# Keeping the two halves of a weight unit in one buffer, and spacing the five buffers by 64 bytes modulo 512

## The chip, the cores and the metric

The kernel runs on one core of one Trainium2 chip. The metric is device time in microseconds (us) of one execution; lower is better.

## The reference

Two layers act on x, 256 rows (SEQ) by 1024 columns (D_MODEL), in float32. Cut to what matters here:

```
for l in range(2):
    h = rms_norm(x, norm_mix_pre[l])
    proj = h @ w_in[l]                         # 1024 x 8224
    y_a = mla_branch(...)   @ w_o_mla[l]       # attention, 8 heads; w_uq, w_ukv inside
    y_b = short_conv_branch(...) @ w_o_sc[l]
    y_c = conformer_branch(...)  @ w_o_cf[l]   # convolution of 31 taps
    y_d = gmlp_branch(...)       @ w_o_gm[l]
    g = sigmoid(gate_logits + gate_b[l])       # four gates
    merged = g0*y_a + g1*y_b + g2*y_c + g3*y_d
    x = x + rms_norm(merged @ w_out[l], norm_mix_post[l])
    h2 = rms_norm(x, norm_ffn_pre[l])
    f_g, f_u = split(h2 @ w_ffn_in[l])         # 1024 x 5632
    x = x + rms_norm((silu(f_g) * f_u) @ w_ffn_out[l], norm_ffn_post[l])
```

## The kernel before

**Tiling.** The 256 rows are two row tiles of 128 (t = 0, 1). All weights stream once from HBM, in units of at most 128 partitions by 2048 float32 (1 MB). `Weights.load` brings a unit into a `raw` tile (4 buffers). `Weights.split` then makes two operands of it for TensorE: ScalarE casts `raw` to float32r, which is `hi`, and VectorE computes `lo = raw - hi`; both work in spans of 1024 columns, so a full unit is two casts and two subtractions. `hi` and `lo` are tiles of their own with 5 buffers each (`B_HI`). Activations are split in the same way, into `hth` and `htl` (the normed input, transposed) and pairs in the common 2 KB tiles (`slot`, 25 buffers: `fh`/`fl`, `mh`/`ml` and so on).

**Products.** `group` issues three matmuls for each 128 rows of contraction: (left hi, right hi), (left hi, right lo), (left lo, right hi). The left operand is loaded into the array, the right one streams through it. In most stages the left operand is an activation and the weights stream, 512 columns a matmul. In `b_unit` the weights are the left operand and 256 columns of `hth`/`htl` stream, so there `hi` is read by the first two matmuls of a triple and `lo` by the third. In `compressed` 272 columns of weights stream. For one layer that is 64 stretches of 24 matmuls with 512 columns (1536), 12 calls of `b_unit` with 48 (576 of 256 columns), 96 of 272 and 24 of 384: 2232, and 4464 for both layers. The other TensorE work is transposes, attention and the gMLP mixing, in plain float32.

**Order.** The order of TensorE's instructions is the order of the code; those of ScalarE, VectorE, GpSimd and SyncE are placed beside it by a planner inside the kernel (`Engine`, `event`, `pump`) from estimated costs. A unit is split when one of the five buffers has been freed (`Weights.free`, `fill`), so five units are ahead of TensorE at most. Waits between engines are derived from the tiles: the first instruction that writes into a reused buffer waits for all readers of what lay there before.

**Addresses.** Every tile starts at some byte of each partition of SBUF. In the built program the start modulo 512 is 64 for `raw`, `hi`, `lo`, `hth`, `htl`, `gain` and all `slot` tiles (`gt`, `m`, `gv`, `brow`, `f` are such tiles), 192 for `x` and the identity, and 352 for the 4 KB tiles `h` of the norms. All `hi` and `lo` buffers are 8192 bytes apart. A span of `compressed` weights starts at a step of 2176 bytes for each 128 rows of contraction and 1088 bytes for the second half, so the streaming operand there begins 0, 64, 128, 192, 256 or 320 bytes (modulo 512) behind the operand loaded into the array; in all other stages that difference is 0.

Of the kernel before, what the change touches and what calls it, by code (L numbers as in the profile page):

```python
# [12 lines left out]
F32R = mybir.dt.float32r  # L13
# [5 lines left out]
P = 128  # L19
# [12 lines left out]
EPS = 1e-6  # L32
NCOL = 148
UW = 2048
FIRST = 544

O_CQ, O_CKV, O_KR = 0, 256, 512
# [59 lines left out]
def hybrid_encoder(ctx: ExitStack, tc: tile.TileContext, wts, x_in, pos, invf, cols, rows, wst, out):  # L97
# [159 lines left out]
    wp = ctx.enter_context(tc.tile_pool(name="wp", bufs=1))  # L257
# [3 lines left out]
    B_RAW, B_HI, B_SLOT, B_BIG, B_GAIN = 4, 5, 25, 2, 2  # L261
# [7 lines left out]
    def nm(s):  # L269
        cnt[0] += 1  # L270
        return f"{s}_{cnt[0]}"
# [49 lines left out]
    class Weights:  # L321
# [4 lines left out]
        def load(self, i, t=0.0):  # L326
            l, u = divmod(i, NU)
            w, after = widths[u], t
            t = wp.tile([P, UW], F32, tag="raw", name=nm("raw"), bufs=B_RAW)
            o = (l * offs[-1] + offs[u]) * P  # L330
            src = wts[o : o + w * P].rearrange("(p w) -> p w", w=w)
            step = FIRST if i == 0 else w
            for c in range(0, w, step):
# [2 lines left out]

        def split(self, i):
            w = widths[i % NU]
            h = wp.tile([P, UW], F32R, tag="hi", name=nm("hi"), bufs=B_HI)
            lo = wp.tile([P, UW], F32R, tag="lo", name=nm("lo"), bufs=B_HI)  # L340
            raw = self.raw.pop(i)
            step = FIRST if i == 0 else 1024
            self.parts[i] = (h, lo)
            spans = [(c, min(w, c + step)) for c in range(0, w, step)]

            def rank():
                return 0 if i <= self.n + NEAR else 3

            for c, e in spans:
                act.copy(h[:, c:e], raw[:, c:e], rank=rank)  # L350
                dve.tensor_tensor(lo[:, c:e], raw[:, c:e], h[:, c:e], op=ALU.subtract, rank=rank, then=self.more if e == w else None)
# [124 lines left out]
    def pre_norm(t, g):  # L476
        h = big()
        ss = small(1)
        r = small(1)
        act.activation(h, x[:, t, :], AF.Square, scale=D ** -0.5, accum_out=ss, rank=FAST)  # L480
        rstd_of(r, ss, rank=FAST)
        for j in range(2):
            c = slice(512 * j, 512 * (j + 1))
            dve.scalar_tensor_tensor(h[:, c], x[:, t, c], r, g[:, c], op0=ALU.mult, op1=ALU.mult, rank=FAST)

        def turn():
            for j in range(2):
                yield need(h)
                b = sbank()
                transposes(b, [h[:, 512 * j + P * k : 512 * j + P * (k + 1)] for k in range(4)])  # L490
                bv = b.rearrange("p (k n) -> p k n", n=P)
                split(hth[:, t, 4 * j : 4 * j + 4, :], htl[:, t, 4 * j : 4 * j + 4, :], bv, FAST)

        return turn()
# [83 lines left out]
    def layer(l):  # L578
# [26 lines left out]
        def mla_tr(t, cn):  # L605
            yield need(cn)
            b = sbank()
            transposes(b, [cn[:, P * k : P * (k + 1)] for k in range(4)])
            for j in range(2):
                o = slice(t * P, (t + 1) * P)  # L610
                split(ft2(qc[j])[:, :, o], ft2(ql[j])[:, :, o], b[:, 256 * j : 256 * (j + 1)].rearrange("p (f n) -> p f n", f=2))
# [84 lines left out]
        def split_op(name, j, src):  # L696
            hi, lo = slot(F32R, name + "h"), slot(F32R, name + "l")
            split(hi, lo, src)
            ops[name][j] = (ft2(hi), ft2(lo))
# [481 lines left out]
```

## Time and profile before

| | |
|---|---|
| median of 2 runs | 966.59 us (966.5 to 966.67) |
| profiled execution, its own time | 966.32 us |
| its span, first to last instruction | 964.5 us |
| TensorE busy | 950.7 us (99% of the span) |
| VectorE busy | 669.5 us |
| ScalarE busy | 476.4 us |
| HBM read | 177.63 MB, 185 GB/s over the span |

The span is what the instruction records cover; 1.8 us of the execution's own time lie outside it. Busy times overlap between engines. Matmuls are pipelined: the record of one lasts longer than its share of the engine, so the rate is read from start to start.

### The profile page before, as it was taken

The numbers are of one execution on the slowest core, as the hardware profiler recorded it, in microseconds if no ns is written. First come the engines' busy times: TensorE is split into PE (matmuls) and PEld (weight loads), VectorE is DVE, ScalarE is ACT, GpSimd is POOL, SyncE is SP. The second block draws the span as 40 slices with busy tenths as digits, with TensorE's granted clock in tenths as the row PEclk, the third lists the DMA queues.
The fourth block names the chain that finished last, engine by engine and source line by source line (L and its number), as shares of the span: only waits on it lengthen the run. The fifth ranks groups of instructions, "written<-read, shape, count | busy, mean of one in ns | idle before, by whom it ended". The sixth has DMA issues, their size and how long they took to land.

```text
span 964.5 us, 12950 instructions
## 1 busy us (share of the span) xinstructions
PE 950.7 (99%) x5098; PEld 821.9 (85%) x5098; DVE 669.5 (69%) x1018; ACT 476.4 (49%) x733; POOL 44.6 (5%) x87
## 2 busy tenths in 40 slices
PE   8999999999999999999999999999999999999997
PEld 7999988888887888888899999888888878888885
DVE  6968788898857655553387888788987485555532
ACT  6656655436435644443275656544455364444421
POOL 1100000000001000000031000000000010000000
PEclk9999999999999999999999999999999999999999
DMA  9844353455844645565267144445566266455601
GB/s 365 291 164 152 114 196 142 179 212 191 321 153 156 237 180 192 195 218 180 88 239 286 56 170 161 147 177 200 213 243 233 104 236 244 175 175 187 227 0 44
DMA packets 29726, 179.52 MB, mean 186 GB/s; under 512 B 3681, under 2 KB 3809, under 8 KB 10209
## 3 DMA queue, kind: packets, MB, share of 16 engines
q1 hardware_dynamic: 29664, 178.69, 51.8%
q8 instruction: 40, 0.66, 0.3%
q14 instruction: 22, 0.17, 0.1%
HBM read 177.63 MB, written 1.05 MB: 185 GB/s over the span
## 4 chain that ended last, share of the span: by engine, by line
PE 94%; DVE 2%; ACT 1%; issue 1%; DMA 1%; POOL 1%; SPq 0%; DVEq 0%; POOLq 0%; ACTq 0%
PE pb L248 74%; PE acc L248 12%; PE psd L252 4%; PE psd L248 2%; PE av L248 1%; DVE lo L175 1%; DMA raw<-in_wts_dram 1%; POOL c L175 1%; ACT hi L175 1%; DVE h L175 0%; ACT h L175 0%; DVE x L175 0%; SPq L309 0%; DVE htl L175 0%; ACT sq L175 0%
## 5 line engine op out<-in xcount | busy, mean ns | idle before, releaser
L175 DVE TENSOR_TENSOR lo<-raw,hi 128x1024 fp32r<-128x1024 f32 (+4 forms) x321 | 374.1, 1202 | 136.3 <-ACT hi L175 136.1
L175 ACT CAST hi<-raw 128x1024 fp32r<-128x1024 f32 (+4 forms) x321 | 319.1, 1037 | 277.2 <-PE pb L248 140.6
L248 PE MATMUL pb<-hi,hth 128*128 128x512 f32 (+1 forms) x704 | 272.5, 387 | 0.8 <-ACT hth L175 0.8
L248 PE MATMUL pb<-lo,hth 128*128 128x512 f32 (+1 forms) x704 | 268.1, 381 | 3.9 <-DVE lo L175 3.9
L248 PE MATMUL pb<-hi,htl 128*128 128x512 f32 (+1 forms) x704 | 268.3, 381 | 0.7 <-DVE htl L175 0.4
L248 PEld LDWEIGHTS pb<-lo,hth 128*128 128x128 f32 x704 | 132.3, 188 | 29.1 <-DVE lo L175 5.2
L248 PEld LDWEIGHTS pb<-hi,htl 128*128 128x128 f32 x704 | 132.2, 188 | 27.2 <-DVE htl L175 2.0
L248 PEld LDWEIGHTS pb<-hi,hth 128*128 128x128 f32 x704 | 132.3, 188 | 24.8 <-ACT hth L175 1.1
L248 PE MATMUL pb<-hth,hi 128*128 128x256 f32 x384 | 109.9, 286 | 0.0
L248 PE MATMUL pb<-htl,hi 128*128 128x256 f32 x384 | 108.6, 283 | 0.0
L248 PE MATMUL pb<-hth,lo 128*128 128x256 f32 x384 | 108.6, 283 | 0.0
L175 DVE SCALAR_TENSOR_TENSOR yc<-zc,hcol,yc 128x241 f32<-128x241 f32 (+14 forms) x240 | 97.8, 472 | 0.0
L248 PEld LDWEIGHTS pb<-htl,hi 128*128 128x128 f32 x384 | 73.7, 192 | 0.3
L248 PEld LDWEIGHTS pb<-hth,hi 128*128 128x128 f32 x384 | 73.6, 192 | 0.3
L248 PEld LDWEIGHTS pb<-hth,lo 128*128 128x128 f32 x384 | 73.7, 192 | 0.0
L248 PE MATMUL acc<-hi,fh 128*128 128x512 f32 x176 | 68.8, 391 | 0.0
L248 PE MATMUL acc<-hi,fl 128*128 128x512 f32 x176 | 68.5, 389 | 0.0
L248 PE MATMUL acc<-lo,fh 128*128 128x512 f32 x176 | 68.5, 389 | 0.0
L248 PEld LDWEIGHTS acc<-hi,fl 128*128 128x128 f32 x176 | 33.0, 188 | 7.0
L248 PEld LDWEIGHTS acc<-hi,fh 128*128 128x128 f32 x176 | 33.0, 188 | 6.8
L248 PEld LDWEIGHTS acc<-lo,fh 128*128 128x128 f32 x176 | 33.0, 188 | 6.7
L175 POOL TENSOR_SCALAR c<-c 128x1 f32<-128x1 f32 (+1 forms) x20 | 12.7, 634 | 518.1 <-ACT sq L175 474.5
(161 smaller groups left out, 1007.6 us busy)
## 6 DMA issues: line engine op xcount, KB each, us to landing
raw<-in_wts_dram SPq DMA_DIRECT2D x152, 1024.0 KB, 4.8
brow<-in_rows_dram SPq DMA_DIRECT2D x24, 256.0 KB, 5.6
gain<-in_rows_dram SPq DMA_DIRECT2D x8, 512.0 KB, 6.1
raw<-in_wts_dram SPq DMA_DIRECT2D x3, 816.0 KB, 4.6
raw<-in_wts_dram SPq DMA_DIRECT2D x2, 768.0 KB, 5.8
raw<-in_wts_dram SPq DMA_DIRECT2D x2, 544.0 KB, 6.1
x<-in_x_dram SPq DMA_DIRECT2D x2, 512.0 KB, 5.9
out_dram<-x SPq DMA_DIRECT2D x4, 256.0 KB, 2.1
```

The lines of the kernel that those rows point to most:

```text
L175: o.emit = lambda: f(*a, **k)
L248: nc.tensor.matmul(out, lhsT, rhs, **k)
L252: nc.tensor.transpose(out=out, in_=in_, identity=identity)
```

## The change

`hi` and `lo` of a unit become the first and the second 2048 columns of one tile `hl` with 5 buffers. A tile is 16 columns (64 bytes) longer than the two together, 16448 bytes, which is 64 modulo 512. In the built program the five buffers start at 64, 128, 192, 256 and 320 modulo 512, and `lo` has the same residue as its `hi`, as before. `raw`, `hth`, `htl`, `x` stay where they were. What is allocated behind the buffers moves 320 bytes up: `gain` and all `slot` tiles from 64 to 384, the tiles `h` from 352 to 160.

```diff
+SHIFT = 16
@@ class Weights, split @@
-            h = wp.tile([P, UW], F32R, tag="hi", name=nm("hi"), bufs=B_HI)
-            lo = wp.tile([P, UW], F32R, tag="lo", name=nm("lo"), bufs=B_HI)
+            both = wp.tile([P, 2 * UW + SHIFT], F32R, tag="hl", name=nm("hl"), bufs=B_HI)
+            h, lo = both[:, :UW], both[:, UW : 2 * UW]
```

The order of the instructions on every engine is the same before and after. What differs is where some waits stand. ScalarE's row, in the `b_unit` stage of layer 0, before (`th` is the tanh of a `b_unit` result `pb`; the casts write weight units into reused buffers):

```order
L175 CAST hi_554<-raw_406 128x1024 [waits DVE_49,DMAHW0_49,PE_49,Activation_49]
L175 ACTIVATE th_556<-pb_485 128x512 [waits PE_49]
L175 CAST hi_554<-raw_406 128x1024
L175 ACT_TABLE_LOAD
L175 ACTIVATE sin<-ang_479 128x32 [waits DVE_49]
```

and the same place after:

```order
L176 CAST hl_544<-raw_398 128x1024 [waits DVE_49,DMAHW0_49,PE_49,Activation_49]
L176 ACTIVATE th_545<-pb_475 128x512
L176 CAST hl_544<-raw_398 128x1024
L176 ACT_TABLE_LOAD
L176 ACTIVATE sin<-ang_469 128x32 [waits DVE_49]
```

Nothing moved; the wait of `th` for TensorE is gone, because the cast ahead of it now waits for the last reader of `lo` as well, which is the last matmul of that `b_unit`. There are 8 such rows on ScalarE; 4 subtractions on VectorE lose their wait for TensorE in the same way, and 8 matmuls gain a wait of TensorE for one of its own earlier matmuls, beside the wait for ScalarE that they have in both kernels. SyncE's and GpSimd's waits are the same.

## Rows read from the trace of the kernel before

**Rows 1.** The page: span, busy times by engine, TensorE's granted clock in 40 slices.
```profile
span 964.5 us, 12950 instructions
PE 950.7 (99%) x5098; PEld 821.9 (85%) x5098; DVE 669.5 (69%) x1018; ACT 476.4 (49%) x733; POOL 44.6 (5%) x87
...
PEclk9999999999999999999999999999999999999999
```

**Rows 2.** The page: the chain that ended last, shares by engine.
```profile
PE 94%; DVE 2%; ACT 1%; issue 1%; DMA 1%; POOL 1%; SPq 0%; DVEq 0%; POOLq 0%; ACTq 0%
```

**Rows 3.** Timeline, TensorE, FFN input stage (start, length, instruction): 94 rows, first and last.
```profile
347.00 0.39 PE L248 MATMUL pb<-hi,htl 128*128 128x512 f32 x1
...
368.08 0.39 PE L248 MATMUL pb<-hi,htl 128*128 128x512 f32 x1
```

**Rows 4.** Timeline, TensorE, FFN output stage: 88 rows, first and last.
```profile
440.16 0.39 PE L248 MATMUL acc<-hi,fh 128*128 128x512 f32 x1
...
459.88 0.39 PE L248 MATMUL acc<-hi,fh 128*128 128x512 f32 x1
```

**Rows 5.** Timeline, TensorE, `b_unit` stage: 54 rows, first and last.
```profile
85.53 0.28 PE L248 MATMUL pb<-hth,lo 128*128 128x256 f32 x1
...
91.89 0.28 PE L248 MATMUL pb<-htl,hi 128*128 128x256 f32 x1
```

**Rows 6.** Timeline, TensorE, `compressed` stage of layer 1: 36 rows, first and last.
```profile
499.49 0.29 PE L248 MATMUL pb<-hi,htl 128*128 128x272 f32 x1
...
503.90 0.29 PE L248 MATMUL pb<-lo,hth 128*128 128x272 f32 x1
```

**Rows 7.** Windows: length, busy PE, PEld, DVE, ACT, POOL, clock, DMA share.
```profile
180.00:295.00 115.00, 115.00 (x529) 95.43 (x528) 90.62 (x127) 53.60 (x78) 3.44 (x9) 1.00 0.57 204
31.00:100.00 69.00, 69.00 (x520) 66.86 (x519) 56.27 (x135) 40.03 (x58) 2.77 (x4) 1.00 0.51 190
314.00:425.00 111.00, 111.00 (x510) 92.23 (x509) 63.01 (x73) 53.05 (x73) 0.00 (x0) 1.00 0.55 196
434.00:479.00 45.00, 45.00 (x200) 37.24 (x200) 16.53 (x16) 14.21 (x18) 1.09 (x4) 1.00 0.42 144
```

**Rows 8.** Groups by shape: busy us, mean ns of one | idle before it.
```profile
L175 DVE TENSOR_TENSOR lo<-raw,hi 128x1024 fp32r<-128x1024 f32 x311 | 368.6, 1220 | 136.3 <-ACT hi L175 136.1
L175 ACT CAST hi<-raw 128x1024 fp32r<-128x1024 f32 x311 | 314.1, 1052 | 275.7 <-PE pb L248 140.6 <-issue 64.1 <-PE acc L248 36.3
...
L175 DVE TENSOR_TENSOR m<-m,gt 128x512 f32<-128x512 f32 x24 | 16.5, 686 | 0.1
...
L175 DVE SCALAR_TENSOR_TENSOR x<-h,c,x 128x512 f32<-128x512 f32 x16 | 11.3, 748 | 9.3 <-POOL c L175 9.3
...
L175 ACT ACTIVATE h<-x 128x1024 f32<-128x1024 f32 x8 | 8.5, 1062 | 11.7 <-DVE x L175 9.4 <-DMA x<-in_x_dram 2.3
...
L175 DVE TENSOR_TENSOR h<-acc,gain 128x512 f32<-128x512 f32 x8 | 5.4, 690 | 25.7 <-ACT sq L175 13.5 <-PE acc L248 12.1
...
L175 DVE SCALAR_TENSOR_TENSOR gv<-gv,c,brow 128x512 f32<-128x512 f32 x4 | 3.0, 748 | 1.2 <-POOL c L175 1.2
```

**Rows 9.** Waits: who for whom, us in total, times, longest.
```profile
ACT hi L175 <- PE pb L248: 140.6, 54, 4.2
...
PE pb L248 <- DVE lo L175: 3.9, 3, 1.5
```

**Rows 10.** Timeline, GpSimd, in the norms around 300 us.
```profile
297.66 0.22 POOL L175 TENSOR_SCALAR c<-c 128x1 f32<-128x1 f32 x1 [6.13 <-ACT sq L175]
...
302.70 2.13 POOL L175 TENSOR_SCALAR c<-c 128x1 f32<-128x1 f32 x1 [3.45 <-ACT h L175]
```

**Rows 11.** Timeline, VectorE, the same place at 300 us.
```profile
301.26 3.49 DVE L175 TENSOR_TENSOR lo<-raw,hi 128x1024 fp32r<-128x1024 f32 x3
305.52 0.75 DVE L175 SCALAR_TENSOR_TENSOR h<-x,c,gain 128x512 f32<-128x512 f32 x1 [0.77 <-POOL c L175]
```

**Rows 12.** Windows, instructions on `lo` alone: PE, PEld, DVE in the gate stage.
```profile
180.00:295.00 115.00, 63.16 (x163) 30.48 (x163) 47.33 (x40) 1.00 0.57 204
```

## The prediction

> **What bounds the kernel now.** I read the page's busy times first, then its chain. TensorE is busy for 950.7 of the 964.5 us of the span, at a granted clock of 9 tenths or more in every slice, and the chain that ended last runs through TensorE for 94% of the span [rows 1, 2]. The other engines have room: VectorE 69%, ScalarE 49%. So the time can move in two ways only: the rate at which TensorE takes matmuls changes, or TensorE comes to wait more or less.
>
> The rate is read from start to start, since the records overlap. With 512 columns streaming it is (368.08 - 347.00)/93 = 226.7 ns in the FFN input stage [rows 3] and (459.88 - 440.16)/87 = 226.7 ns in the FFN output stage [rows 4]. With 256 columns it is (91.89 - 85.53)/53 = 120.0 ns [rows 5], with 272 columns (503.90 - 499.49)/35 = 126.0 ns [rows 6]. At the granted clock of 1.00 [rows 7], which is the upper level of 2.4 GHz, the columns alone take 213.3, 106.7 and 113.3 ns. A fixed 13.4, 13.3 and 12.7 ns a matmul remains, whatever the column count. Over the 4464 float32r matmuls this fixed part is some 59 us, the only large sum in the trace that an address could possibly own.
>
> Waiting is small: TensorE stood idle for VectorE's `lo` for 3.9 us in all, in 3 places [rows 9].
>
> The changed kernel's own profiled execution is compared with 966.32 us (964.5 of span and 1.8 around it); the median of the runs is 966.59, 0.3 higher, and the forecast below is given on the median's scale.
>
> **The change part by part.**
>
> *Instructions.* None is added, removed or moved: the order on each engine is the same. Sum: 0. SyncE's waits are the same too, so no load is issued in another place.
>
> *Addresses against TensorE's reads.* Four of the five buffers now start 64 to 256 bytes (modulo 512) away from `hth`, and all five away from the `slot` tiles, where before everything lay at 64. The trace of before has a stage with just such distances: in `compressed` the streaming operand is 0 to 320 bytes off the loaded one, and there the fixed part is 12.7 ns instead of 13.3 to 13.4. So a distance is worth at most 0.6 to 0.7 ns a matmul, 0.65 x 4464 = 2.9 us. I take 0: starts are recorded with a few ns of rounding, 272 columns is a third size, and a mean over 35 matmuls at six distances that still lies within 1 ns of the rest says that the distance isn't what the 13 ns are. I keep -2.9 for the range.
>
> *Addresses against the writes of ScalarE and VectorE.* Casts and subtractions write one buffer while TensorE reads another. If they collided, the rate would depend on how much they run. In the FFN input stage VectorE is busy for 57% and ScalarE for 48% of the time, in the output stage for 37% and 32% [rows 7], and the rate is 226.7 ns in both [rows 3, 4]. Moreover a shift of the start can't keep the streams apart: a cast moves 4096 bytes in 1052 ns [rows 8], 3.9 bytes a ns, and TensorE reads 2048 in 226.7 ns, 9.0 bytes a ns, so the distance between them runs through all 512 residues every 100 ns or so, wherever they start. Sum: 0.
>
> The one contention that the trace does show has nothing to do with addresses. GpSimd's one-column addition takes 0.22 us at 297.66 and 2.13 us at 302.70 [rows 10], where three subtractions run back to back on VectorE [rows 11]. The Trainium skill, page "SBUF — State Buffer", section "Who interferes with whom", says that only the port pair which VectorE shares with GpSimd causes contention, as a lock held for a whole instruction, that a VectorE instruction with two SBUF inputs takes part in it, and that TensorE and ScalarE wait for nobody. The 2.13 against 0.22 us agrees. By that rule no address matters, which speaks against any gain of this change, and the sum stays 0.
>
> *Within one instruction.* In a subtraction `raw` stays at 64 while `hi` and `lo` move together; in a cast input and output part. Here streams go at one speed and keep their distance. Pairs of rows bound it: VectorE takes 748 ns for 512 columns with operands at 352 and 192 (`x<-h,c,x`) and 748 with all at 64 (`gv<-gv,c,brow`); 690 with output at 352 and one input in PSUM (`h<-acc,gain`) and 686 with all at 64 (`m<-m,gt`); ScalarE takes 1062 ns for 1024 columns from 192 to 352 (`h<-x`) and 1052 from 64 to 64 [rows 8]. That is 0 to 8 ns for 1024 columns on VectorE and up to 10 on ScalarE, or 2.5 and 3.1 us over 311 of each, in either direction as far as the rows can exclude it. Both engines lie beside TensorE there (in the gate stage VectorE is busy for 90.6 of 115 us), so on the path it is 0. If that cover were gone, all 2.5 us would count; I keep +2.5.
>
> *Waits.* After a `b_unit`, the cast into its buffer waits for the last reader of `lo`, one matmul of 120 ns later than the last reader of `hi`. There are 12 calls of `b_unit` a layer, 24 in all: 24 x 0.12 = 2.9 us at most, on ScalarE. Behind the cast on ScalarE stand `th` or `gu` (which need the same last matmul anyway), then the second cast; behind these the subtraction, and TensorE only five units later. ScalarE waits there for TensorE anyway (140.6 us in 54 places, rows named ACT hi), while TensorE hardly waits for `lo` [rows 9]. On the path: 0, at worst +2.9. The 8 added waits of TensorE for its own matmuls name work of an earlier use of the same bank; each stands beside a wait for ScalarE, which had to read that bank's finished sum, so it is fulfilled already. The 12 waits that go were fulfilled by the cast's own. Sum: 0.
>
> *Timing by chance.* Where GpSimd is locked out, VectorE then stands idle for 0.77 us before the norm's `h`, and TensorE is idle there too [rows 11]; the other layer has the same place. A shift of a cast by some 0.1 us could free both or lock another norm: -1.5 to +1.5 us. I take 0, since nothing in that stage moves.
>
> Total: 0, from -2.9 - 1.5 to +2.9 + 1.5 at the bounds, and these are not likely to come together.
>
> **The rivals.**
>
> *The 13 ns are a meeting of the two operands' addresses.* With every operand at one residue, loading the next left operand might get in the way of the stream at each matmul, and the new distances would free it. Price: the 13.3 ns of all matmuls but those with `hth` and the one buffer that stays at 64; if half the matmuls use `hth` and a fifth of these keep distance 0, 0.9 x 59 = 53 us, 913 us. For it: the fixed part exists in all stages where the distance is 0. Against it: `compressed` has five other distances and the same fixed part within 0.7 ns [rows 6]. The Trainium skill, page "TensorE: Matmul & The Clock Gate", section "Wait — 56ns, not 53.3ns?", has a fixed cost of about 2.5 ns a matmul; as an estimate by that page some 11 of the 13 ns here would be avoidable, 48 us in all, and the trace doesn't agree with it for float32r in any stage.
>
> *VectorE becomes the bound (the slow side).* If a subtraction whose two inputs differ in residue had to take its columns twice, it would last 1.07 us longer (1220 - 686 = 534 ns for 512 columns more [rows 8], so 1068 ns for 1024). Place: the gate stage, with 40 subtractions in 115 us [rows 12]. It decides from (115 - 90.6)/40 = 0.61 us more per subtraction; at 1.07 us VectorE needs 90.6 + 42.8 = 133.4 us, 18.4 over, and 37 us in both layers: 1003 us. Against it: `x<-h,c,x` with two residues costs the same 748 ns as `gv<-gv,c,brow` with one.
>
> *The later cast counts in full:* 966.6 + 2.9 = 969.5 us, slower but within 2%. For it, that casts wait for TensorE at all; against it, the five units of lead.
>
> *The change doesn't separate what meets.* `hi` and `lo` keep one common residue, and the buffer being written differs from the one being read by 64 bytes that the two speeds run through anyway. Then the time is that of the forecast; I count it there.
>
> **How the numbers follow.** Likeliest is no change, 966.6 us, with its bounds 0.86. The gain on TensorE's fixed part has 0.03, and a smaller gain of some us that no row shows 0.04; the later cast or a slightly slower rate beyond the bound has 0.05; VectorE as the bound 0.02. The range is the forecast's own, 2.9 us to either side, which leaves out less than 2 in 10: 963.7 to 969.5. A run of this kernel can tell some 2% (19 us) from no change: faster by more than that 0.03, slower 0.02, within 0.95.
>
> **What the profile after would show.** Starts 226.7, 120.0 and 126.0 ns apart in the stages of rows 3 to 6, a subtraction of 1220 and a cast of 1052 ns, and the same pieces of waiting around 300 and 775 us. A rate of 225 ns or less with 512 columns would prove the address argument wrong, in favour of the first rival. A subtraction over 1240 ns would say that the distance within an instruction costs something; TensorE waiting for `lo` more than 3.9 us, that the lead of five units was not the cover I took it for.

## The result and the profile after

The changed kernel takes 975.14 us (975.11 to 975.17, 2 runs) against 966.59 before: ratio 1.0089, 95% interval [1.0067, 1.011]. It is slower by 8.6 us, within 2% but clear of its interval and outside the forecast's range.

The page of the kernel after, span, busy times and TensorE's clock:

```profile
span 973.4 us, 12958 instructions
PE 959.5 (99%) x5098; PEld 819.3 (84%) x5098; DVE 670.2 (69%) x1018; ACT 476.2 (49%) x733; POOL 44.5 (5%) x87
...
PEclk9999999999999999999999999999999999999999
```

Against [rows 1] the span has grown by 8.9 us and TensorE's busy time by 8.8; VectorE, ScalarE and GpSimd are within 1 us, the clock is the same. So TensorE does the same work more slowly, and it doesn't wait more. The groups by shape and the waits of the kernel after say the same:

```profile
L176 DVE TENSOR_TENSOR hl<-raw,hl 128x1024 fp32r<-128x1024 f32 x311 | 368.5, 1220 | 140.2 <-ACT hl L176 139.8
L176 ACT CAST hl<-raw 128x1024 fp32r<-128x1024 f32 x311 | 313.6, 1050 | 281.5 <-PE pb L249 152.8 <-issue 65.3 <-PE acc L249 37.2
```

```profile
PE pb L249 <- DVE hl L176: 3.4, 3, 1.5
```

A subtraction takes 1220 ns as before, a cast 1050 instead of 1052 [rows 8]; TensorE waits 3.4 us for `lo` instead of 3.9 [rows 9]. GpSimd's blocked addition is still there (timeline, GpSimd):

```profile
304.41 2.13 POOL L176 TENSOR_SCALAR c<-c 128x1 f32<-128x1 f32 x1 [3.45 <-ACT h L176]
```

What changed is the time from one matmul's start to the next, and it changed from buffer to buffer. The timeline of TensorE in the FFN output stage, the first matmul of each of five units, 24 matmuls apart (a row can merge two matmuls with the same names):

```profile
433.65 0.63 PE L249 MATMUL acc<-hl,fh 128*128 128x512 f32 x2
...
439.12 0.63 PE L249 MATMUL acc<-hl,fh 128*128 128x512 f32 x2
...
444.71 0.62 PE L249 MATMUL acc<-hl,fh 128*128 128x512 f32 x2
...
450.29 0.62 PE L249 MATMUL acc<-hl,fh 128*128 128x512 f32 x2
...
455.78 0.39 PE L249 MATMUL acc<-hl,fh 128*128 128x512 f32 x1
```

These units lie in the buffers at 128, 320, 256 and 192 (modulo 512), and `fh`/`fl` at 384. The differences divided by 24 are 227.9, 232.9, 232.5 and 228.8 ns, where all of [rows 4] had 226.7. The weights, which stream, begin 0, 192, 128 and 64 bytes behind the activations, which are loaded, modulo 256. This difference of start addresses, streaming minus loaded operand, modulo 256 bytes, is called the distance below.

In `b_unit` the same happens the other way. The timeline of TensorE, the second matmul of two triples in each of three calls:

```profile
84.08 0.28 PE L249 MATMUL pb<-htl,hl 128*128 128x256 f32 x1
...
89.06 0.28 PE L249 MATMUL pb<-htl,hl 128*128 128x256 f32 x1
...
89.77 0.28 PE L249 MATMUL pb<-htl,hl 128*128 128x256 f32 x1
...
94.53 0.28 PE L249 MATMUL pb<-htl,hl 128*128 128x256 f32 x1
...
95.59 0.28 PE L249 MATMUL pb<-htl,hl 128*128 128x256 f32 x1
...
99.55 0.28 PE L249 MATMUL pb<-htl,hl 128*128 128x256 f32 x1
```

Over 42, 42 and 33 matmuls that is 118.6, 113.3 and 120.0 ns, at distances of 128, 192 and 0 bytes between the streaming `hth`/`htl` and the loaded weights; [rows 5] had 120.0.

Taken over the whole trace, each start put to the addresses of its operands in the built program (starts further apart than 260 ns with 512 columns and 150 ns with 256, which are waits and changes of stage, left out of the means):

| distance, bytes | 0 | 64 | 128 | 192 |
|---|---|---|---|---|
| 512 columns: matmuls, mean ns | 959, 228.6 | 576, 229.9 | 672, 232.3 | 864, 233.2 |
| 256 columns: matmuls, mean ns | 432, 119.9 | 192, 116.6 | 288, 118.6 | 240, 115.4 |

The distance counts, and not the tile: at 192 it is 233.4 ns with `hth` loaded and the buffer at 256, and 233.5 with `fh` loaded and the buffer at 64, where the rhythm is steady (inside a stretch of one distance, away from its ends and from waits). 256 bytes more change nothing: with `hth` loaded, steady starts lie 227.5 ns apart with the buffer at 64 and 227.3 with the buffer at 320. With 256 columns the distance alone doesn't fix the rate: of the four calls at 64, one runs at 113.3 ns and three at 117.6 to 117.9, and the mean of 116.6 is none of these. Summed start to start, the 512-column matmuls take 718.3 us instead of 707.6 (+10.7), the 256-column ones 137.3 instead of 139.4 (-2.1); the rest adds 0.3. That is the 8.9 us of the span.

### The profile page after: what moved, and what is told of

Read it like the earlier page. It is cut to its first block, busy times and chain, and to the rows that moved or that the text cites. A ratio compares the mean times of both kernels' runs of the same rounds, so it can differ in the third digit from the quotient of the medians.

```text
span 973.4 us, 12958 instructions
## 1 busy us (share of the span) xinstructions
PE 959.5 (99%) x5098; PEld 819.3 (84%) x5098; DVE 670.2 (69%) x1018; ACT 476.2 (49%) x733; POOL 44.5 (5%) x87
## 4 chain that ended last, share of the span: by engine, by line
PE 94%; DVE 2%; DMA 1%; ACT 1%; issue 1%; POOL 1%; SPq 0%; DVEq 0%; POOLq 0%; ACTq 0%
PE pb L249 74%; PE acc L249 13%; PE psd L253 4%; PE psd L249 2%; PE av L249 1%; DMA raw<-in_wts_dram 1%; DVE hl L176 1%; POOL c L176 1%; ACT hl L176 1%; DVE h L176 0%; SPq L310 0%; DVE x L176 0%; ACT h L176 0%; DVE htl L176 0%; ACT sq L176 0%
## 5 line engine op out<-in xcount | busy, mean ns | idle before, releaser
L176 DVE TENSOR_TENSOR hl<-raw,hl 128x1024 fp32r<-128x1024 f32 (+4 forms) x321 | 374.2, 1202 | 140.3 <-ACT hl L176 139.8
L176 ACT CAST hl<-raw 128x1024 fp32r<-128x1024 f32 (+4 forms) x321 | 318.6, 1035 | 283.3 <-PE pb L249 152.8
L249 PE MATMUL pb<-hl,hth 128*128 128x512 f32 (+1 forms) x1408 | 428.8, 387 | 4.6 <-DVE hl L176 3.4
L249 PEld LDWEIGHTS pb<-hl,hth 128*128 128x128 f32 x1408 | 258.1, 188 | 57.4 <-DVE hl L176 4.7
L249 PE MATMUL pb<-hl,htl 128*128 128x512 f32 (+1 forms) x704 | 270.2, 384 | 0.6 <-DVE htl L176 0.4
L249 PEld LDWEIGHTS pb<-hl,htl 128*128 128x128 f32 x704 | 132.2, 188 | 29.5 <-DVE htl L176 1.9
L249 PE MATMUL pb<-hth,hl 128*128 128x256 f32 x768 | 139.3, 282 | 0.0
L249 PEld LDWEIGHTS pb<-hth,hl 128*128 128x128 f32 x768 | 118.9, 189 | 0.3
L249 PE MATMUL acc<-hl,fh 128*128 128x512 f32 x352 | 110.2, 394 | 0.0
L249 PE MATMUL pb<-htl,hl 128*128 128x256 f32 x384 | 107.9, 281 | 0.0
```

The source lines that it names most:

```text
L176: o.emit = lambda: f(*a, **k)
L249: nc.tensor.matmul(out, lhsT, rhs, **k)
```

## The experiments

Theory A: TensorE's rate depends on the distance between the operand that streams and the operand that is loaded. Its rivals: B, the common buffer costs (later release, other waits); C, the distance between the buffer being written and the one being read costs; D, the streaming operand meets what ScalarE and VectorE write. Theory A has two forms: in A1 the operand that counts is the one being loaded for the next matmul beside the stream, in A2 it is the matmul's own, loaded before. Each time stands beside its own chip's 966.5 to 966.6 us of the kernel before.

### hi and lo in one buffer, no spacing

```diff
-SHIFT = 16
+SHIFT = 0
```

> hi and lo in one buffer, but without the 16 extra columns: all five buffers at 64 modulo 512, as hth, htl, raw and the slot tiles. Theory A (TensorE's rate depends on the distance, modulo 256 bytes, between the streaming operand and the operand loaded into the array): 966.6 us, 512-column matmuls 226.7 ns apart, 256-column ones 120.0. Theory B (the common buffer costs, through the later release of hi and the other waits): some 975 us with the rates of before.

Measured: 966.52 us, ratio 0.9999 [0.999, 1.0009]. B falls: the common buffer with all its moved waits is free, as the prediction had it. All of the loss is the spacing's. The casts of this kernel and TensorE's wait for `lo`:

```profile
L176 ACT CAST hl<-raw 128x1024 fp32r<-128x1024 f32 x311 | 314.0, 1051 | 276.2 <-PE pb L249 144.8 <-issue 64.3 <-PE acc L249 36.3
...
PE pb L249 <- DVE hl L176: 3.9, 3, 1.5
```

ScalarE stands idle 0.5 us longer before its casts than in [rows 8], and TensorE's wait for `lo` is that of [rows 9].

### All five buffers at one distance of 128 bytes

```diff
-SHIFT = 16
+SHIFT = 64
-            h, lo = both[:, :UW], both[:, UW : 2 * UW]
+            o = 32
+            h, lo = both[:, o : o + UW], both[:, UW + o : 2 * UW + o]
```

The buffers are a multiple of 256 bytes long now, so that they, the `slot` tiles and `gain` keep the residue 64 modulo 256; only `o` moves the weights.

> All five buffers at one common distance of 128 bytes (modulo 256) from hth, htl, raw and the slot tiles; nothing apart between the buffers. Theory A, from the rows of the changed kernel at this distance (232.5 ns with 512 columns, 118.6 with 256): 3072 x 5.8 ns more and 1152 x 1.4 ns less, 966.6 + 17.8 - 1.6 = 983 us. Theory C (what costs is that a buffer being written lies 64 bytes apart, modulo 512, from the one being read): 966.6 us, since the five buffers differ by multiples of 256 only. Theory B: some 975 us.

Measured: 980.69 us, ratio 1.0146 [1.0131, 1.0161]. C falls, since nothing is apart between the buffers and the loss is larger than in the changed kernel. The chain that ended last, a stretch of 96 matmuls of the FFN input stage of this kernel (start, us, what):

```profile
350.86 22.30 PE pb L249 x96
```

That is 232.3 ns a matmul. Over the trace steady rhythms have 232.5 ns with 512 columns and 119.1 with 256. The time is 2 us under the expectation; the sum of the 512-column starts grew by 15.2 us instead of 17.8, because only the 2659 steady ones grew, by 15.0 us; the other 412, near transposes, waits and changes of stage, grew by 0.2. With 256 columns 0.9 us came off instead of 1.6.

### 64 bytes for b_unit alone

```diff
+            o = 16 if units[i % NU][1:3] == (0, D) else 0
```

(with `SHIFT = 64` and the slices of the experiment before, as in all that follow; the condition picks the units that `b_unit` loads into the array.)

> Buffers at the distance 0 (modulo 256) for all units but those of b_unit, which lie 64 bytes further up in their buffer, so that the streaming hth begins 192 bytes (modulo 256) behind the loaded weights. Theory A, from the rows of the changed kernel (115.0 ns against 120.0): 1152 x 5.0 ns less, 966.6 - 5.8 = 961 us, faster than both kernels. Theories B and C: not faster than 966.6 us.

Measured: 962.39 us, ratio 0.9957 [0.9942, 0.9971]: faster than both kernels, but by 4.2 us instead of 5.8. The trace has two steady rhythms at this distance: 8 of the 24 calls of `b_unit` run at 113.3 to 114.0 ns, the others at 117.6 to 117.9. The timeline of TensorE in one call of each kind, the second matmul of the first and last triple, 45 matmuls apart:

```profile
43.49 0.28 PE L249 MATMUL pb<-htl,hl 128*128 128x256 f32 x1
...
48.79 0.28 PE L249 MATMUL pb<-htl,hl 128*128 128x256 f32 x1
...
514.77 0.28 PE L249 MATMUL pb<-htl,hl 128*128 128x256 f32 x1
...
519.87 0.28 PE L249 MATMUL pb<-htl,hl 128*128 128x256 f32 x1
```

That is 117.8 and 113.3 ns, with the same addresses modulo 256.

### Scan in steps of 16 bytes

```diff
+            o = 4 * ((i % NU + 4 * (i // NU)) % 16)
```

> A scan in one run: each unit lies 0, 16, 32 ... 240 bytes into its buffer, in turn. Theory A: the start-to-start time of the matmuls is a function of the distance modulo 256 alone, the same in every stage with that column count: with 512 columns 226.7, 229, 232.5 and 233.4 ns at 0, 64, 128 and 192 bytes, with 256 columns 120.0, 116.6, 118.6 and 115.0 at 0, 64, 128 and 192; what lies between is open. Theories B and C: no order by distance. Total about 970 us either way.

Measured: 979.16 us in one run. Steady mean ns from start to start by distance, worked out as above:

```
bytes      0    16    32    48    64    80    96   112   128   144   160   176   192   208   224   240
512 col 227.4 231.6 233.4 233.1 229.5 231.1 233.6 231.4 232.5 233.3 234.3 232.6 233.3 234.6 233.4 230.8
256 col 119.9 117.4 116.6 116.7 117.8 118.1 120.1 119.1 120.1 120.2 117.3 118.7 113.3 117.8 118.4 118.3
```

The order by distance is there and repeats the values at 64, 128 and 192 within 0.4 ns with 512 columns; with 256 columns 1.2, 1.5 and 2.1 ns of difference say that a mean hides several rhythms. The total was missed by 9 us: I had the distances between the multiples of 64 near the mean of these, and nearly all are at the upper end. With 512 columns nothing beats 0.

### htl alone moved by 128 bytes

```diff
-    htl = cp.tile([P, T, KD, P], F32R, name="htl")
+    htl = cp.tile([P, T * KD * P + 64], F32R, name="htl")[:, 32 : 32 + T * KD * P].rearrange("p (t k n) -> p t k n", t=T, k=KD)
```

> The kernel before, with htl alone moved 128 bytes (modulo 256); hth, weights and everything else keep one residue. It asks which pair meets. A triple is (hth, hi), (hth, lo), (htl, hi), loaded operand first. Theory A1 (a stream is slowed by the loading of the next matmul's operand, which runs beside it): with 512 columns the second matmul of a triple takes some 232.5 ns, the first and third 226.7. Theory A2 (a stream is slowed by its own loaded operand): the third takes 232.5, the others 226.7. Theory D (the streaming operand meets what ScalarE and VectorE write, and the loaded operand is nothing to it): 226.7 in all three. In both A1 and A2 640 matmuls get 5.8 ns more, 966.6 + 3.7 = 970 us, less up to 1 us in b_unit; in D 966.6.

Measured: 971.13 us, ratio 1.0048 [1.0025, 1.0071]. D falls: no weight buffer and no write into one has moved against another (what lies behind `htl` moved by 256 bytes). Of the triples in the stages with `hth` (523 of each place, steady) the first takes 227.1 ns, the second 232.5, the third 234.1; with the other activations all stay at 226.5 to 227.7. So A1 holds, the matmul beside which `htl` is loaded is slowed, and the one that then runs with `htl` is slowed too, as A2 has it. Whether the third is slowed by its own operand or by its slowed neighbour, this run doesn't separate; in the scan of `lo` below, matmuls are slowed whose own pair lies at distance 0. The timeline of this kernel shows how near the two are, TensorE's streams (PE) and loads (PEld):

```profile
348.33 0.40 PE L248 MATMUL pb<-hi,hth 128*128 128x512 f32 x1
348.33 0.19 PEld L248 LDWEIGHTS pb<-lo,hth 128*128 128x128 f32 x1
348.56 0.39 PE L248 MATMUL pb<-lo,hth 128*128 128x512 f32 x1
348.56 0.19 PEld L248 LDWEIGHTS pb<-hi,htl 128*128 128x128 f32 x1
348.79 0.39 PE L248 MATMUL pb<-hi,htl 128*128 128x512 f32 x1
```

The load for the next matmul starts within 4 ns of the stream of this one, in 99% of the matmuls with 512 columns. So stream and load meet in the same way at each matmul of a stretch, which would let their start addresses matter; that this is the reason is argued, not shown.

### Scan in steps of 4 bytes

```diff
+            o = (i % NU + 4 * (i // NU)) % 16
```

> A second scan: each unit lies 0, 4, 8 ... 60 bytes into its buffer. Theory A with a unit of 16 bytes: the 512-column time is one value within each group of 16 bytes, 227 ns for 0 to 12 bytes, about 231.6 at 16 to 28, 233 at 32 to 60. Theory A without such a unit: it rises from the first 4 bytes on. Total about 979 us. No step is expected below 226.

Measured: 979.68 us in one run. Steady means with 512 columns:

```
bytes      0     4     8    12    16    20    24    28    32    36    40    44    48    52    56    60
512 col 226.8 238.1 233.2 228.9 231.8 239.0 234.3 228.6 233.4 235.4 233.6 230.0 233.3 236.0 232.0 228.5
```

Three units in a row, at 0, 4 and 8 bytes, the first matmul of each, 24 matmuls apart (timeline, TensorE):

```profile
400.98 0.62 PE L249 MATMUL pb<-hl,hth 128*128 128x512 f32 x2
...
406.43 0.63 PE L249 MATMUL pb<-hl,hth 128*128 128x512 f32 x2
...
412.14 0.63 PE L249 MATMUL pb<-hl,hth 128*128 128x512 f32 x2
```

That is 227.1 ns at 0 and 237.9 at 4. A group of 16 bytes doesn't have one value: within each 16 bytes it falls from 4 to 12, by 9 to 10 ns in the first two groups and 5 to 8 in the others. Again 0 is best. With 256 columns the lowest mean was 113.7 ns, at 52 bytes up in the buffer (distance 204).

### Scan of lo's distance

```diff
+            o = 16 if units[i % NU][1:3] == (0, D) else 0
+            q = max(o, 4 * ((i % NU + 4 * (i // NU)) % 16))
+            h, lo = both[:, o : o + UW], both[:, UW + q : 2 * UW + q]
```

> hi lies as in the kernel with 64 bytes for b_unit alone, lo lies 0, 16 ... 240 bytes further (from 64 on in b_unit). Theory A1 or A2: with 512 columns only one or two matmuls of a triple change with lo's distance, to 231 to 234 ns; total 962.4 + some 1000 matmuls x 6 ns = 968 us. If some combination of unequal distances runs under 226 ns with 512 columns or holds 113.3 ns with 256, it shows here.

Measured: 976.77 us in one run, 9 over the expectation. With 512 columns all three matmuls of a triple grow in most distances (at 48 bytes to 233.0, 237.3 and 234.1 ns), although `hi` lies at 0: a displaced `lo` spoils its neighbours' rhythm too. No triple's mean is under the 227.3 of distance 0. In `b_unit`, with `hi` 64 and `lo` 192 bytes up, a triple averages 114.1 ns in one call.

### 52 bytes for b_unit

`o = 13` instead of 16 in the third experiment.

> As the kernel with 64 bytes for b_unit alone, but 52 bytes instead of 64, so that the streaming hth begins 204 bytes (modulo 256) behind the loaded weights; all other units at distance 0. In the scan of 4-byte steps this distance held 113.7 ns in all its rows, where 192 bytes switched between 113.3 and 117.8. Theory A: 1152 x (120.0 - 113.7) = 7.3 us less than before, 959.3 us, and 3 us less than with 64 bytes. If the 113 ns were only a matter of how the stage is entered, it gives about the 962.4 us of 64 bytes.

Measured: 964.84 us, ratio 0.9977 [0.9968, 0.9987]: theory A's 959.3 us failed, and the 962.4 of the other expectation was missed too. One distance again gives two rhythms, as the doubt in its last sentence had it. The timeline of TensorE in two calls of this kernel, the second matmul of the first and last triple counted:

```profile
90.48 0.28 PE L249 MATMUL pb<-htl,hl 128*128 128x256 f32 x1
...
95.16 0.28 PE L249 MATMUL pb<-htl,hl 128*128 128x256 f32 x1
...
112.74 0.28 PE L249 MATMUL pb<-htl,hl 128*128 128x256 f32 x1
...
115.83 0.28 PE L249 MATMUL pb<-htl,hl 128*128 128x256 f32 x1
```

39 matmuls at 120.0 ns, 27 at 114.4 (the first few of these still settle, the rest run at 113.3), at one and the same distance. 18 of the 24 calls hold the slow rhythm. The ten runs fall into two lots as well, 963.2 to 963.4 and 964.7 to 965.2 us.

### 8 bytes for b_unit

`o = 2`.

> As the kernel with 64 bytes for b_unit alone, with 8 bytes instead: the streaming hth begins 248 bytes (modulo 256) behind the loaded weights. In the scan of 4-byte steps this distance gave 115.6 ns in its two calls of b_unit, one in each layer. If the distance alone sets the time: 1152 x 4.4 ns less than before, 961.5 us. If the entry into the stage chooses among several steady rhythms here too, anything from 961 to 966.5 us, with calls of one kernel differing.

Measured: 961.70 us, ratio 0.995 [0.9935, 0.9964]. All 24 calls run at 115.5 to 116.0 ns: here no second rhythm showed.

### hi 64 and lo 192 bytes up in b_unit

```diff
+            o = 16 if units[i % NU][1:3] == (0, D) else 0
+            q = 48 if units[i % NU][1:3] == (0, D) else 0
+            h, lo = both[:, o : o + UW], both[:, UW + q : 2 * UW + q]
```

> b_unit with hi 64 and lo 192 bytes into the buffer, all other units at distance 0. In the scan of lo's distance this pair ran at 114.1 ns in the one call that had it. If the pair of distances alone sets the time: 1152 x 5.9 ns less than before, 959.8 us. If the entry chooses, as with 52 bytes, up to 966.5 us, and calls differ.

Measured: 959.37 us, ratio 0.9925 [0.9909, 0.9942], the fastest of all. The timeline, one call:

```profile
88.20 0.28 PE L249 MATMUL pb<-htl,hl 128*128 128x256 f32 x1
...
92.62 0.28 PE L249 MATMUL pb<-htl,hl 128*128 128x256 f32 x1
```

39 matmuls at 113.3 ns, and all 24 calls have 113.3 to 114.4 on average. The 256-column starts sum to 132.2 us instead of 139.4: the 7.2 us of the gain.

## Why the prediction was wrong

**The step that failed** is "Addresses against TensorE's reads". It bounded what a distance is worth by -0.65 ns a matmul, 2.9 us in all and only as a gain, from the mean of `compressed` [rows 6], and took 0. Measured, a distance costs up to 12 ns with 512 columns (226.8 to 239.0) and saves up to 6.7 ns with 256 (120.0 to 113.3). In the changed kernel that is +10.7 and -2.1 us, and with the rest +8.9 us of span.

Two things were wrong in the reading. First, 272 columns were taken for 512, and this decided. Sorted by distance, the starts in `compressed` of the kernel before (both layers, those under 140 ns apart) lie 126.9 ns apart at 0, 125.3 at 64, 126.6 at 128 and 125.1 at 192: no distance is dearer than 0 there, so a sorted reading would have found a small gain too, and no loss. With 512 columns nearly every distance costs. Second, the mean over six distances hid that the addresses act at all: single starts in that stretch lie 120 to 130 ns apart, in an order that repeats. Of the signs that the prediction named, only a faster rate spoke against its address argument; a slower one had a share of the chance of 0.05, beside the later cast.

**The first rival** had the right pair, the streaming and the loaded operand, and the wrong sign and price: it expected one residue for all to be the worst case. For 512 columns it is the best that any run here found; for 256 columns it is not, and the most that comes off there is 6.7 of the 13.3 ns. The argument against it, again from rows 6, was the failed step once more. Its price also took half the matmuls to use `hth`, where 3264 of the 4464 use `hth` or `htl`; by that its sum would have been 50 us instead of 53. The Trainium skill, page "SBUF — State Buffer", section "Who interferes with whom", gives TensorE two read ports of its own and calls them independent. The runs don't bear this out for the rate, which depends on the addresses that the two read: with the common buffer it is 966.5 us when both operands start at one residue, and 980.7 us when the weights lie 128 bytes off (first two experiments).

**Addresses against the writes** was right: with one distance and one buffer layout nothing is left for the writes (first two experiments), and D fell in the fifth. The reason given there, that streams of different speed run through all residues, was not tested by itself. It could not have been carried over to TensorE's own stream and load, which start together (fifth experiment).

**Instructions, waits, order** were right in the sum: 966.52 us with the common buffer alone. "None is added" was not exact: the page counts 12958 instructions instead of 12950 [rows 1], the 8 more being the added waits on TensorE, in that experiment too. The later cast, bounded by 2.9 us on ScalarE, is seen there as 0.5 us of idle time, off the path. TensorE's wait for `lo` is even 0.5 us shorter in the changed kernel. **Within one instruction** was right: 1220 and 1050 ns. **Timing by chance** was right in that nothing of it showed: the additions of 2.13 us are where they were. VectorE did not become a bound (a subtraction takes 1220 ns), and the later cast cost nothing in the total.

**The fourth rival**, that the change doesn't separate what meets, was half true. It is no help to say that `hi` and `lo` keep one residue: what meets is the weights and the activations, and these it did separate.

What stays open is the cause inside TensorE or SBUF; no run looked there. Shown is that the start addresses of the two operands set the rate: with 512 columns it follows their distance modulo 256, whichever tile is loaded. With 256 columns something else takes part, since one distance allows two rhythms (113.3 and 117.8 ns at 64 and at 192 bytes, 113.3 and 120.0 at 204). What chooses between them is open too; calls in a row mostly keep the rhythm, so the entry into a stage is likely, not shown.

## What to carry to other kernels

On a kernel that TensorE bounds, the start addresses of the streaming and of the loaded operand are a parameter: in this one, equal modulo 256 bytes was best where 512 float32r columns stream, and shorter streams had to be measured, stage by stage and more than one call of each. Read the rate from start to start, by stage and by operand address, and look at the single values before a mean is used as a bound. Do not carry a bound from one column count to another: here 272 columns showed none of the loss that 512 showed. Where a layout is changed for one pair of accesses, list every pair that it moves; here five buffers were spread among themselves, and what counted was their distance from the activations.

## What the runs showed of the hardware that was not expected

- 512 float32r columns start 226.8 ns apart with both operands at one address modulo 256, and 228.5 to 239.0 at all other distances tried in steps of 4 and 16 bytes (two scans, one run each); 4 and 20 bytes are the worst (238.1 and 239.0).
- 256 columns start 120.0 ns apart at distance 0 and 113.3 at best; at distances of 64, 192 and 204 bytes a whole call holds one of two rhythms, at 248 bytes all 24 calls have 115.5 to 116.0.
- 272 columns start 125.1 to 126.9 ns apart at distances of 0, 64, 128 and 192 bytes.
- With `hi` and `lo` at two different distances (192 and 64 bytes) the fast rhythm of 113.3 ns holds in all 24 calls (113.3 to 114.4 on average), which neither the run with 64 nor the one with 52 bytes for both did.
